# A transformer block on one Trainium2 core: the first residual norm is taken out of the chain to the router

## Chip, cores and metric

One core of one Trainium2 chip runs the whole block as one launch. The metric is device time in microseconds (us), the median of three runs; lower is better. A profile of one execution stands beside the times; all times of instructions below come from it and count from the start of its span.

## The reference, cut to what matters

Sequence 256, width 2048, 32 experts in 4 groups, two experts per token, everything in 32-bit floats.

```python
sh1, sc1, g1, sh2, sc2, g2 = split(silu(c) @ w_ada + b_ada, 6)
u = layer_norm(x) * (1 + sc1) + sh1
mix = token_mixer(u, ...) # attention and gated delta rule, ends in merged @ w_out
x = layer_norm(ALPHA * x + g1 * mix, ln1_g, ln1_b) # the first residual norm
u = layer_norm(x) * (1 + sc2) + sh2 # a second norm, without gain
ffn = hier_moe(u, ...) # router logits u @ [w_group | w_expert], top 2, expert MLPs
x = layer_norm(ALPHA * x + g2 * ffn, ln2_g, ln2_b)
```

So between the projection by `w_out` and the router stand two layer norms, one behind the other, each with a mean and a variance over 2048 columns.

## The kernel before

Tokens lie on the partitions in NT = 2 halves `x[t]` of 128 x 2048. The output projection (`out_todo`) runs over four chunks c of 512 columns; each is 8 half tiles of weights, split into a high and a low part by ScalarE (`wh`) and VectorE (`wl`), and multiplied three times. `evac(c, ps)` takes a finished chunk from PSUM: times the gate row, plus ALPHA times x, statistics by `bn_stats` into `sb`. After chunk 0 it asks for the two rows of the norm, `l1[0]` (gain) and `l1[1]` (bias), each broadcast into a 1 MB buffer; `router_prep` folds the modulation `sc2c` into the router's weights `wr` and `sh2c` into its bias.

After the projection `both` turns the statistics into mean and 1/deviation. Then, for every chunk and half, VectorE normalises x in place (L1059 subtracts the mean and multiplies by the gain, L1060 scales and adds the bias), TensorE transposes the result (L1063), ScalarE copies it out (`uq`) and sums its squares (L1066), and `logits(c)` multiplies it by `wr` (L1053). A copy and a product with `wsel` (L1072, L1075) turn the logits back; small VectorE operations finish the second norm on the logits `L` and choose the experts. ScalarE writes `xh`, the second norm's rows (L1101). For the first pair of experts `slots` makes one-hot columns `G` (L1208), and `gather` multiplies `xh` by them, a quarter (`step(kq)`) of the 16 blocks at a time: two products per block into one PSUM tile, then four modulations into `XT`. Quarter 0 precedes the first `gate_up`; quarters 1 to 3 stand in it ahead of k = 2, 6 and 10 (`GS`).

An expert pair takes 24 weight tiles of 1 MB through the SP queue: 16 for `gate_up`, 8 for `down`. SP issues in order, each load as soon as its buffer is free. There are 17 buffers: 4 (`wp`, L74), 6 (`wm`, L1325) and 7 (`wm1`, L1338). In `wm1` two are first the rows `l1` and five hold the first five gate_up tiles, loaded during the projection (`load_ahead`). Tiles 5 to 8 go to `wp`, 9 to 14 to `wm`, tile 15 and the first six tiles of `down` to `wm1`, and so on round the ring.

The order of instructions on an engine is a planner's: of those ready by its own clock it takes the one that stands first in the program. An instruction that is pinned (`To`, `Vo`, `So`) stays behind the one traced before it on its engine.

Of the kernel before, what the change touches and what calls it, by code (L numbers as in the profile page):

```python
# [37 lines left out]
GS = (2, 6, 10)  # L38
# [25 lines left out]
def tile_block(ctx: ExitStack, tc: tile.TileContext, A: dict, out: bass.AP, dbg=None, upto=99):  # L64
# [855 lines left out]
    rw = rwx.enter_context(tc.tile_pool(name="rw", bufs=1, side=R, reuse_waits="tile"))  # L920
    ahead = []

    def load_ahead():
        n = len(ahead)
        w = wm1.tile([P, 2048], F32, tag="w1", name="w1")
        nc.sync.dma_start(w, A["w_gu"][n])
        ahead.append(w)
# [46 lines left out]
    l1 = []  # L974
# [7 lines left out]
    def router_prep():  # L982
        mod2 = rw.tile([P, KT, 2], F32, name="mod2")
# [5 lines left out]
        V.tensor_tensor(wr, wr, sc2c.unsqueeze(2).to_broadcast([P, KT, 64]), op=MUL)  # L989
        G.memset(wr[:, :, 36:37], 1.0)  # L990
        V.tensor_add(wsel, ident[:, 0:37], ident[:, 64:101])
        rc = rw.tile([36, 2], F32, name="rcol")
        V.tensor_copy(rc, pb[:36, 0:2])
        pb = ps_w.tile([P, 512], F32, tag="ws", name="pbr2")
        for j in range(2):
            T.matmul(pb[:, 64 * j:64 * j + 36], rc[:, j:j + 1].to_broadcast([36, P]), ident[:36, :36],
                     start=True, stop=True)
        V.tensor_tensor(br, pb[:, :36], RI("br"), op=ADD)
        V.tensor_scalar(ncs, pb[:, 64:100], -1.0, None, op0=MUL)

    def g2_rows(cs):
        for c in cs:
            p = ps_w.tile([P, 512], F32, tag="ws", name=f"g2{c}")
            spread(p, mrs[5], 32 * c)
            SC.copy(g2b[:, c * 512:(c + 1) * 512], p)

    def evac(c, ps):
        cs = slice(c * 512, (c + 1) * 512)
        for t in range(NT):
# [15 lines left out]

# [12 lines left out]

    for _ in ada:
        pass  # L1040
    mv, rs = both(sb, "b")
    s2 = mo.tile([P, NT, 4], F32, name="s2")
    nb1 = mo.tile([P, 1], F32, name="nb1")
    V.tensor_reduce(nb1, l1[1], axis=AX.X, op=ADD)
    V.tensor_scalar(nb1, nb1, -1.0 / D, None, op0=MUL)
    pl = ps_w.tile([P, 512], F32, tag="ws", name="pl")
    uqs = []

    def logits(c):
        for k in range(4):  # L1050
            K = 4 * c + k
            j = 64 * (k % 2)
            T.matmul(pl[j:j + 64, :S], wr[:, K, :], uqs[c][:, k, :], start=(K < 2), stop=(K >= KT - 2))  # L1053

    for c in range(4):
        cs = slice(c * 512, (c + 1) * 512)
        uq = rw.tile([P, 4, S], F32, tag="uq", name=f"uq{c}", bufs=2)
        for t in range(NT):
            V.scalar_tensor_tensor(x[t][:, cs], x[t][:, cs], mv[:, t, 0:1], l1[0][:, cs], op0=SUB, op1=MUL)  # L1059
            V.scalar_tensor_tensor(x[t][:, cs], x[t][:, cs], rs[:, t], l1[1][:, cs], op0=MUL, op1=ADD)  # L1060
            p = pg(f"ut{t}{c}")
            for k in range(4):
                T.transpose(p[:, k * P:(k + 1) * P], x[t][:, (4 * c + k) * P:(4 * c + k + 1) * P], ident)  # L1063
            SC.copy(uq[:, :, t * P:(t + 1) * P], p.rearrange("p (k s) -> p k s", k=4))
            scr = rw.tile([P, 512], F32, tag="mt", name=f"sq{c}{t}", bufs=2)
            SC.activation(scr, x[t][:, cs], AF.Square, bias=nb1, accum_out=s2[:, t, c:c + 1])  # L1066
        uqs.append(uq)
        if c:
            logits(c - 1)
    logits(3)  # L1070
    lt = rw.tile([P, S], F32, name="lt")
    SC.copy(lt, pl[:, :S])  # L1072
    pl = ps_w.tile([P, 512], F32, tag="ws", name="plt")
    for t in range(NT):
        T.matmul(pl[:, 64 * t:64 * t + 37], lt[:, t * P:(t + 1) * P], wsel, start=True, stop=True)  # L1075
    for t in range(NT):
        dump(f"x1{t}", x[t])

    mv, dv, sv, rs = [mo.tile([P, NT, 1], F32, name=f"{n}c") for n in ("mv", "dv", "sv", "rs")]
    V.tensor_reduce(sv[:, :, 0], s2, axis=AX.X, op=ADD)  # L1080
    py = pl[:, 0:128].rearrange("p (t c) -> p t c", t=NT)[:, :, 36:37]
    V.tensor_scalar(dv, py, 1.0 / D, nb1, op0=MUL, op1=ADD)
    V.tensor_scalar(mv, py, 1.0 / D, None, op0=MUL)
    V.tensor_tensor(dv, dv, dv, op=MUL)
    V.scalar_tensor_tensor(sv, sv, 1.0 / D, dv, op0=MUL, op1=SUB)
    SC.activation(rs, sv, AF.Sqrt, bias=epsl)
    V.reciprocal(rs, rs)
    for t in range(NT):
        V.scalar_tensor_tensor(L[:, t, :], ncs, mv[:, t, 0:1], pl[:, 64 * t:64 * t + 36], op0=MUL, op1=ADD)
        V.scalar_tensor_tensor(L[:, t, :], L[:, t, :], rs[:, t], br, op0=MUL, op1=ADD)  # L1090
# [9 lines left out]
    for t in range(NT):  # L1100
        SC.activation(xh[t], x[t], AF.Identity, bias=nmr[:, t], scale=rs2[:, t])  # L1101
        g2_rows((2 * t, 2 * t + 1))
# [53 lines left out]
    for t in range(NT):  # L1156
# [4 lines left out]
        V.scalar_tensor_tensor(pos[:, t, :], msk[:, t, :], -4096.0, p[:, :NE], op0=MUL, op1=ADD)  # L1161

# [66 lines left out]
    def gather(pr, Gs):  # L1229
        XT = mo.tile([P, KT, P], F32, tag="XT", name=f"XT{pr}")  # L1230

        def step(kq):
            p = pm(f"xg{pr}_{kq}")
            for k in range(4):
                for t in range(NT):
                    T.matmul(p[:, k * P:(k + 1) * P], xh[t][:, (4 * kq + k) * P:(4 * kq + k + 1) * P],  # L1236
                             Gs[t].bitcast(F32), start=(t == 0), stop=(t == NT - 1))
            for k in range(4):
                K = 4 * kq + k
                if kq % 2:  # L1240
# [359 lines left out]
```

## Time and profile before

| what | us |
|---|---|
| three runs, median (lowest to highest) | 1811.14 (1809.91 to 1812.76) |
| the profiled execution, its own time | 1810.3 |
| its span in the profile | 1808.4 |
| last product of the projection starts | 822.77 |
| first product of the first gate_up starts | 853.05 |

The rows further down come from the page of this execution and from questions to its trace. A row of a timeline has start, length, engine, line, operation, output<-inputs, number of instructions; in brackets the engine's idle time before it and what ended it. PEld is TensorE's weight load; each 32-bit product shows as two records of PE and of PEld.

### The profile page before, as it was taken

The page shows a single profiled execution, that of the slowest core. Times are in us where ns is not written, and L with a number is a line of the kernel's source. Part 1 is how long each engine was busy: PE and PEld are TensorE (multiplying, and loading weights), DVE is VectorE, ACT ScalarE, POOL GpSimd, SP SyncE. Part 2 cuts the span into 40 slices and gives each one's busy share as a digit, 9 for nine tenths or more (in the row PEclk, how much of TensorE's full clock was granted, in tenths as well). Part 3 has the DMA queues.
Part 4 walks back from the last instruction along what each step waited for, and adds up shares of the span by engine and source line. Part 5 has one row for each costly group of instructions (what it writes and reads, how often), then busy time and mean ns, then how long its engine had stood idle before and what let it go on. Part 6 is the DMA issues. An engine that isn't in the chain of part 4 may idle for free. (4 is left out here: it accounts for less than half of the span.)

```text
span 1808.4 us, 27501 instructions
## 1 busy us (share of the span) xinstructions
PE 1726.9 (95%) x11526; PEld 1106.4 (61%) x11526; DVE 895.6 (50%) x1454; ACT 516.9 (29%) x955; POOL 43.4 (2%) x50
## 2 busy tenths in 40 slices
PE   7999998999999999997999999999999999999995
PEld 4779887898999999885434444344434444343331
DVE  3356897798788788666223322233213321233026
ACT  3334798336333544435100110011100110011101
POOL 0000001103000000000000000000000000000000
PEclk8999998999999999999999999999999999999998
DMA  9995565465788688978999999999999999999995
GB/s 397 420 362 209 199 254 192 163 258 205 282 288 319 233 303 317 364 263 323 368 421 420 421 420 420 421 421 420 420 421 420 421 420 421 420 420 421 394 422 223
DMA packets 87287, 628.58 MB, mean 348 GB/s; under 512 B 9828, under 2 KB 9828, under 8 KB 11252
## 3 DMA queue, kind: packets, MB, share of 16 engines
q1 hardware_dynamic: 86832, 626.43, 86.4%
q8 instruction: 92, 1.51, 0.3%
q10 hardware_dynamic: 328, 0.36, 0.1%
q14 instruction: 35, 0.29, 0.0%
HBM read 624.65 MB, written 2.10 MB: 347 GB/s over the span
## 5 line engine op out<-in xcount | busy, mean ns | idle before, releaser
L1257 PE MATMUL pg<-w,XT 128*64 128x512 f32 x1024 | 278.5, 599 | 3.4 <-DMA w<-in_w_gu 2.5
L1257 PE MATMUL pu<-w,XT 128*64 128x512 f32 x1024 | 275.5, 594 | 0.0
L293 PE MATMUL ws<-uh,wh 128*128 128x256 f32 x896 | 259.4, 290 | 2.3 <-ACT wh L288 2.3
L288 ACT CAST wh<-w 128x1024 fp32r<-128x1024 f32 x176 | 184.6, 1050 | 257.3 <-PE ws L294 122.2
L295 PE MATMUL ws<-uh,wl 128*128 128x256 f32 x896 | 254.0, 284 | 4.3 <-DVE wl L289 4.3
L294 PE MATMUL ws<-ul,wh 128*128 128x256 f32 x896 | 253.7, 283 | 0.0
L289 DVE TENSOR_TENSOR wl<-w,wh 128x1024 fp32r<-128x1024 f32 x176 | 218.7, 1243 | 52.4 <-PE mx L294 22.8
L1295 PE MATMUL pd<-w,hT 128*64 128x512 f32 x1016 | 234.1, 599 | 0.8 <-DVE hT L1272 0.8
L1264 DVE TENSOR_TENSOR hs<-hs,pu 128x512 f32<-128x512 f32 x16 | 11.0, 687 | 430.3 <-PE pu L1257 430.3
L293 PEld LDWEIGHTS ws<-uh,wh 128*128 128x128 f32 x896 | 169.3, 189 | 12.4 <-issue 7.8
L295 PEld LDWEIGHTS ws<-uh,wl 128*128 128x128 f32 x896 | 169.1, 189 | 6.6 <-DVE wl L289 5.7
L236 DVE SCALAR_TENSOR_TENSOR acc<-w,csil,acc 128x1024 f32<-128x1024 f32 x128 | 165.3, 1307 | 12.6 <-DMA w<-in_w_ada 12.3
L294 PEld LDWEIGHTS ws<-ul,wh 128*128 128x128 f32 x896 | 169.3, 189 | 1.4 <-issue 1.2
L1257 PEld LDWEIGHTS pu<-w,XT 128*64 128x64 f32 x1024 | 77.8, 137 | 146.6 <-issue 146.6
L1257 PEld LDWEIGHTS pg<-w,XT 128*64 128x64 f32 x1024 | 72.5, 137 | 133.6 <-issue 114.0
L1236 PEld LDWEIGHTS xg<-G,xh 128*128 128x128 f32 x1024 | 120.0, 193 | 41.3 <-issue 25.8
L1295 PEld LDWEIGHTS pd<-w,hT 128*64 128x64 f32 x1016 | 66.4, 136 | 124.1 <-issue 109.2
L1236 PE MATMUL xg<-G,xh 128*128 128x128 f32 x1024 | 131.7, 283 | 6.9 <-DVE x L1312 3.5
L1263 ACT ACTIVATE hs<-pg 128x512 f32<-128x512 f32 x16 | 9.6, 598 | 438.5 <-PE pg L1257 438.5
L410 ACT CAST dh<-pd 128x512 fp32r<-128x512 f32 x64 | 37.6, 587 | 281.3 <-DVE pd L1298 160.8
L1298 DVE SCALAR_TENSOR_TENSOR pd<-pd,wsl,g2b 128x512 f32<-128x512 f32 x64 | 48.5, 758 | 104.0 <-PE pd L1295 104.0
L1312 DVE TENSOR_TENSOR x<-x,cb 128x512 f32<-128x512 f32 x120 | 76.9, 682 | 22.7 <-PE cb L1308 22.7
(391 smaller groups left out, 2363.8 us busy)
## 6 DMA issues: line engine op xcount, KB each, us to landing
w<-in_w_gu SPq DMA_DIRECT2D x256, 1024.0 KB, 19.8
w<-in_w_dn SPq DMA_DIRECT2D x127, 1024.0 KB, 19.8
w<-in_w_ada SPq DMA_DIRECT2D x64, 1024.0 KB, 5.1
w<-in_w_in SPq DMA_DIRECT2D x56, 1024.0 KB, 5.1
wx<-in_w_a SPq DMA_DIRECT2D x18, 1024.0 KB, 11.1
w<-in_w_pab SPq DMA_DIRECT2D x16, 1024.0 KB, 6.0
w<-in_w_out SPq DMA_DIRECT2D x16, 1024.0 KB, 4.9
w<-in_w_a SPq DMA_DIRECT2D x14, 1024.0 KB, 10.7
```

The source lines that it names most:

```text
L236: V.scalar_tensor_tensor(acc[:, hc], w[:, hc], csil[:, k:k + 1], acc[:, hc], op0=MUL, op1=ADD)
L288: SC.copy(h, w)
L289: V.tensor_tensor(lo, w, h.bitcast(F32), op=SUB)
L293: T.matmul(p, a[0], b[0], start=first, stop=False)
L294: T.matmul(p, a[0], b[1], start=False, stop=False)
L295: T.matmul(p, a[1], b[0], start=False, stop=last)
L410: SC.copy(h, src)
L1236: T.matmul(p[:, k * P:(k + 1) * P], xh[t][:, (4 * kq + k) * P:(4 * kq + k + 1) * P], Gs[t].bitcast(F32), start=(t == 0), stop=(t == NT - 1))
L1257: T.matmul(dst[64 * e:64 * e + 64, :], XT[:, k, 64 * e:64 * e + 64], we[:, e * 1024 + hv * 512:e * 1024 + hv * 512 + 512], start=(k == 0), ...
L1295: T.matmul(pd[64 * e:64 * e + 64, :], hT[:, f, 64 * e:64 * e + 64], we[:, (2 * (f % 2) + e) * 512:(2 * (f % 2) + e + 1) * 512], start=(f = ...
L1298: V.scalar_tensor_tensor(pd, pd, ws, g2b[:, cs], op0=MUL, op1=MUL)
L1312: V.tensor_tensor(x[t][:, cs], x[t][:, cs], p, op=ADD)
```

## The change

The first norm is no longer applied before the router. In `evac` every chunk is reduced by the mean of its first chunk, `mu0`, and multiplied by the gain at once; ScalarE sums the squares there. The transposes and logit products are taken from these scaled rows. They are pinned: behind the projection's last product, one chunk and half after the other, each pair of transposes and logits in its turn. The logits are now 39 columns wide with tokens on the partitions: 36 for the router, and three (ones, gain, bias) from which small VectorE operations correct the mean, the deviation and the bias afterwards, with constants `cons` that `router_prep` computes by 16 + 4 more small products, after chunk 0 now. The transposed `lt` and `wsel` go.

`xh` is not written ahead of the first gather. `first_gather` multiplies x by one-hot columns scaled by `ag`, and adds a third product per block: three rows (gain, bias, ones) times `r3`. Behind each quarter VectorE finishes the rows of x with `l1[0]` and `l1[1]` and ScalarE writes `xh` for the other pairs. The quarters stand ahead of k = 1, 3, 5. The five `wm1` buffers for the first gate_up tiles are reserved first, the two for `l1` after them. The rows `g2b` are made ahead of the top-2 choice, not after `xh`.

```diff
-GS = (2, 6, 10)
+GS = (1, 3, 5)
@@
+    early = [wm1.tile([P, 2048], F32, tag="w1", name="w1") for _ in AHEAD]
@@ load_ahead
-        w = wm1.tile([P, 2048], F32, tag="w1", name="w1")
-        nc.sync.dma_start(w, A["w_gu"][n])
+        nc.sync.dma_start(early[n], A["w_gu"][n])
@@ (moved up from evac, c == 0)
+    for q in (0, 4):
+        w = wm1.tile([P, D], F32, tag="w1", name=f"l1{q}")
+        nc.sync.dma_start(w, A["lnr"][q:q + 4, :].rearrange("a b -> (a b)").partition_broadcast(P))
+        l1.append(w)
@@ router_prep
+        for k in range(KT):
+            T.matmul(pb[:39, 0:3], wr[:, k, :39], wr[:, k, 36:39], start=(k == 0), stop=(k == KT - 1))
+        V.tensor_copy(rc[:, 0:3], pb[:39, 0:3])
+        for j in range(4):
+            T.matmul(pb[:, 64 * j:64 * j + 39], rc[:, j:j + 1].to_broadcast([39, P]), ident[:39, :39],
+                     start=True, stop=True)
@@ new
+    def turn_part(c, t):
+        uqs[c, t] = rw.tile([P, 4, P], F32, tag="uq", name=f"uq{c}{t}", bufs=4)
+        p = ps_w.tile([P, 512], F32, tag="ws", name=f"ut{t}{c}")
+        for k in range(4):
+            To.transpose(p[:, k * P:(k + 1) * P], x[t][:, (4 * c + k) * P:(4 * c + k + 1) * P], ident)
+        SC.copy(uqs[c, t], p.rearrange("p (k s) -> p k s", k=4))
+
+    def logits(c, t):
+        for k in range(4):
+            K = 4 * c + k
+            To.matmul(pt[t], uqs[c, t][:, k, :], wr[:, K, :39], start=(K == 0), stop=(K == KT - 1))
@@ evac
+            if c == 0:
+                V.bn_aggr(mu0[:, t, :], sb[:, t, 0:1])
+            V.scalar_tensor_tensor(x[t][:, cs], x[t][:, cs], mu0[:, t, 0:1], l1[0][:, cs], op0=SUB, op1=MUL)
+            SC.activation(mt, x[t][:, cs], AF.Square, accum_out=s2[:, t, c:c + 1])
@@ after the projection
+    for i, u in enumerate(units_):
+        turn_part(*u)
+        if i == 4:
+            mv, rs = both(sb, "b")
+        if i:
+            logits(*units_[i - 1])
+    logits(*units_[-1])
     for _ in ada:
         pass
+    g2_rows(range(4))
@@ 15 small VectorE operations, then
+    SC.activation(rs2, sv, AF.Sqrt, bias=epsl)
+    stt(lambda t: L[:, t, :], lambda t: cons[:, 0, :36], nm, lambda t: pa[:, t, :36])
+    V.reciprocal(rs2, rs2)
+    stt(lambda t: L[:, t, :], lambda t: L[:, t, :], rs2, lambda t: br)
@@
-    for t in range(NT):
-        SC.activation(xh[t], x[t], AF.Identity, bias=nmr[:, t], scale=rs2[:, t])
-        g2_rows((2 * t, 2 * t + 1))
+    G.memset(xh[1][:3], 1.0)
+    nc.scalar.dma_start(xh[1][:2], A["lnr"][0:8].rearrange("(q c) b -> q (c b)", q=2))
@@ new, for pair 0
+    def first_gather(Gs):
+        for t in range(NT):
+            V.tensor_scalar(Gp[:, t], Gs[t].bitcast(F32), ag[:, t], None, op0=MUL)
+        for t in range(NT):
+            To.matmul(p[:3, :P], vk[:, t], Gs[t].bitcast(F32), start=(t == 0), stop=(t == NT - 1))
+        SC.copy(r3, p[:3, :P])
+        def products(p, kq, k):
+            for t in range(NT):
+                To.matmul(p, x[t][:, K], Gp[:, t], start=(t == 0), stop=False)
+            To.matmul(p, xh[1][:3, K], r3, start=False, stop=True)
+        def step(kq):
+            ...
+            for t in range(NT):
+                V.scalar_tensor_tensor(x[t][:, cs], l1[0][:, cs], nd[:, t], x[t][:, cs], op0=MUL, op1=ADD)
+                V.scalar_tensor_tensor(x[t][:, cs], x[t][:, cs], rsb[:, t], l1[1][:, cs], op0=MUL, op1=ADD)
+                SC.activation(xh[t][:, cs], x[t][:, cs], AF.Identity, bias=nmr[:, t], scale=rs2[:, t])
@@ gate_up
-                    T.matmul(dst[64 * e:64 * e + 64, :], XT[:, k, 64 * e:64 * e + 64],
+                    (To if step is not None and k < 8 else T).matmul(dst[64 * e:64 * e + 64, :], XT[:, k, 64 * e:64 * e + 64],
```

## Rows read from the trace of the kernel before

**Rows 1.** The page, the span in 40 equal slices: busy share of the DMA engines in tenths, and what they moved.

```profile
DMA  9995565465788688978999999999999999999995
GB/s 397 420 362 209 199 254 192 163 258 205 282 288 319 233 303 317 364 263 323 368 421 420 421 420 420 421 421 420 420 421 420 421 420 421 420 420 421 394 422 223
```

**Rows 2.** Stretches of 5 us: from:to, length, then busy time (and instructions) of PE, PEld, DVE, ACT, POOL, the granted clock of TensorE as a share of 2.4 GHz, the DMA engines' busy share, GB/s.

```profile
845.00:850.00 5.00, 2.60 (x19) 2.23 (x18) 2.66 (x22) 4.98 (x4) 0.00 (x0) 0.98 0.47 193
850.00:855.00 5.00, 4.50 (x22) 3.05 (x23) 1.55 (x10) 2.50 (x8) 0.00 (x0) 0.68 0.01 2
855.00:860.00 5.00, 5.00 (x30) 2.28 (x28) 1.37 (x4) 0.00 (x0) 0.00 (x0) 1.00 0.74 270
...
895.00:900.00 5.00, 5.00 (x41) 4.21 (x42) 2.79 (x9) 1.51 (x4) 0.00 (x0) 1.00 0.50 210
900.00:905.00 5.00, 5.00 (x26) 1.72 (x24) 2.35 (x7) 0.59 (x1) 0.00 (x0) 1.00 0.58 226
...
1780.00:1785.00 5.00, 4.85 (x22) 1.73 (x20) 3.83 (x6) 0.45 (x2) 0.00 (x0) 1.00 0.44 179
```

**Rows 3.** Timeline of the SP queue, the issues of weight loads around the first pair of experts, asked in short stretches: start, us spent issuing, line, load.

```profile
835.94 0.33 SPq L1338 DMA_DIRECT2D w<-in_w_gu  x1
837.26 0.33 SPq L1338 DMA_DIRECT2D w<-in_w_dn  x1
855.11 0.33 SPq L1338 DMA_DIRECT2D w<-in_w_dn  x1
856.82 0.33 SPq L1338 DMA_DIRECT2D w<-in_w_dn  x1
...
865.15 0.33 SPq L74 DMA_DIRECT2D w<-in_w_dn  x1
869.00 0.33 SPq L74 DMA_DIRECT2D w<-in_w_dn  x1
...
886.58 0.33 SPq L1338 DMA_DIRECT2D w<-in_w_gu  x1
900.73 0.33 SPq L1338 DMA_DIRECT2D w<-in_w_gu  x1
```

**Rows 4.** Timeline of all engines between the projection's end and the first gate_up, in order of time.

```profile
823.09 1.06 PE L241 MATMUL ada<-acc,cst 128*32 128x512 f32 x8
...
829.20 2.74 DVE L1060 SCALAR_TENSOR_TENSOR x<-x,rsb,l 128x512 f32<-128x512 f32 x4
...
830.00 3.29 PE L1063 MATMUL ut<-cst,x 128*128 128x128 f32 x16 [5.85 <-DVE x L1060]
...
837.15 0.86 PEld L1063 LDWEIGHTS ut<-cst,x 128*128 128x128 f32 x8 [0.38 <-issue]
...
840.15 0.37 ACT L1072 COPY lt<-pl 128x256 f32<-128x256 f32 x1 [0.52 <-PE pl L1053]
...
841.25 0.22 DVE L1082 TENSOR_SCALAR dvc<-plt,nb 128x2 f32<-128x2 f32 x1 [1.43 <-PE plt L1075]
...
841.74 0.16 DVE L1085 SCALAR_TENSOR_TENSOR svc<-svc,dvc 128x2 f32<-128x2 f32 x1
...
842.46 0.42 DVE L1090 SCALAR_TENSOR_TENSOR L<-L,rsc,br 128x36 f32<-128x36 f32 x2
...
848.24 4.31 PE L1236 MATMUL xg<-G,xh 128*128 128x128 f32 x22 [0.57 <-DVE G L1208]
...
848.82 3.44 PEld L1236 LDWEIGHTS xg<-G,xh 128*128 128x128 f32 x20 [0.31 <-ACT xh L1101]
...
852.54 1.51 ACT L1244 ACTIVATE XT<-xg,sh2c,sc2c 128x128 f32<-128x128 f32 x4
...
853.05 1.15 PE L1257 MATMUL pg<-w,XT 128*64 128x512 f32 x4 [0.50 <-ACT XT L1244]
...
858.13 1.37 DVE L1241 TENSOR_SCALAR XT<-xg,sc2c,sh2c 128x128 f32<-128x128 f32 x4 [5.23 <-PE xg L1236]
```

**Rows 5.** Timeline of TensorE inside and just behind the first gate_up: a gather quarter, and products of 32 columns with 128 x 128 weights.

```profile
865.04 2.05 PE L1236 MATMUL xg<-G,xh 128*128 128x128 f32 x16
867.02 1.08 PE L1257 MATMUL pg<-w,XT 128*64 128x512 f32 x4
...
886.47 0.63 PE L1195 MATMUL cnt<-msk,cst 128*128 128x32 f32 x4
886.94 0.41 PE L1219 MATMUL gt<-cst,G 128*128 128x128 f32 x2
```

**Rows 6.** Timeline of TensorE where chunk 0 of the projection has ended and VectorE is at `evac`.

```profile
756.42 0.61 PE L293 MATMUL mx<-wh,mh 128*128 128x512 f32 x2
756.87 1.02 PE L168 MATMUL g<-mr,cst 128*128 128x512 f32 x2
757.82 1.28 PE L988 MATMUL pbr<-mod,rin 128*36 128x2 f32 x32
759.03 0.50 PE L294 MATMUL mx<-wl,mh 128*128 128x512 f32 x1
```

**Rows 7.** Timeline of VectorE at the same place: the weight splits that follow `evac`.

```profile
757.03 2.35 DVE L289 TENSOR_TENSOR wl<-w,wh 128x1024 fp32r<-128x1024 f32 x2
```

**Rows 8.** The page's list of the costliest groups, the casts of the weight splits: busy time, mean ns of one, then ScalarE's idle time just before them and what ended most of it.

```profile
L288 ACT CAST wh<-w 128x1024 fp32r<-128x1024 f32 x176 | 184.6, 1050 | 257.3 <-PE ws L294 122.2
```

**Rows 9.** The page's list of DMA issues: KB each, median us from issue to landing.

```profile
out<-x SPq DMA_DIRECT2D x2, 256.0 KB, 2.5
```

More of the change, by code (lines that the diff above doesn't have):

```diff
@@ L924, in load_ahead @@
         n = len(ahead)
-        w = wm1.tile([P, 2048], F32, tag="w1", name="w1")
-        nc.sync.dma_start(w, A["w_gu"][n])
-        ahead.append(w)
+        nc.sync.dma_start(early[n], A["w_gu"][n])
+        ahead.append(early[n])
     def out_todo():
@@ L960, in tile_block @@
     sb = mo.tile([P, NT, 4, 6], F32, name="sb")
+    s2 = mo.tile([P, NT, 4], F32, name="s2")
+    mu0 = mo.tile([P, NT, 2], F32, name="mu0")
+    nb1 = mo.tile([P, 1], F32, name="nb1")
     g2b = mo.tile([P, D], F32, name="g2b")
@@ L988, in router_prep @@
             T.matmul(pb[:36, 0:2], wr[:, k, :36], mod2[:, k, :], start=(k == 0), stop=(k == KT - 1))
-        V.tensor_tensor(wr, wr, sc2c.unsqueeze(2).to_broadcast([P, KT, 64]), op=MUL)
+        rc = rw.tile([39, 4], F32, name="rcol")
+        G.memset(rc, 0.0)
+        V.tensor_copy(rc[:36, 3:4], pb[:36, 0:1])
+        V.tensor_tensor(wr[:, :, :36], wr[:, :, :36], sc2c.unsqueeze(2).to_broadcast([P, KT, 36]), op=MUL)
         G.memset(wr[:, :, 36:37], 1.0)
-        V.tensor_add(wsel, ident[:, 0:37], ident[:, 64:101])
@@ L1024, in evac @@
             router_prep()
+        if c == 2:
+            SC.activation(epst, epsl, AF.Sqrt)
+    epst = mo.tile([P, 1], F32, name="epst")
     g1_row(0)
@@ L1037, in both @@
         return mv, rs
+    pt = [pg(f"pl{t}")[:, :39] for t in range(NT)]
+    units_ = [(c, t) for c in range(4) for t in range(NT)]
+    for i, u in enumerate(units_):
[5 more added lines that the diff above has]
+    logits(*units_[-1])
     for _ in ada:
         pass
[L1041 to L1057, printed above, removed]
-        for t in range(NT):
[L1059 to L1073, printed above, removed]
-    for t in range(NT):
[L1075 to L1090, printed above, removed]
@@ new lines, in stt @@
+    def stt(dst, a, sc, b):
+        for t in range(NT):
+            V.scalar_tensor_tensor(dst(t), a(t), sc[:, t], b(t), op0=MUL, op1=ADD)
+    one = lambda a: (lambda t: a[:, t])
+    col = lambda j: (lambda t: pt[t][:, j:j + 1])
+    pcol = lambda j: (lambda t: pa[:, t, j:j + 1])
+    stt(one(q2), col(37), nd, one(sv))
+    stt(one(pa), lambda t: cons[:, 1], nd, lambda t: pt[t])
+    stt(one(pa), one(pa), rs, lambda t: cons[:, 2])
+    stt(one(q2), one(q2), rs, col(38))
+    V.tensor_scalar(nm, pa[:, :, 36:37], -1.0 / D, None, op0=MUL)
@@ L1248, in gate_up, with spread_out @@
+    def spread_out(XT, p, kq):
+        for k in range(4):
+            K = 4 * kq + k
+            if kq % 2:
+                V.tensor_scalar(XT[:, K, :], p[:, k * P:(k + 1) * P], sc2c[:, K:K + 1], sh2c[:, K:K + 1],
+                                op0=MUL, op1=ADD)
+            else:
+                SC.activation(XT[:, K, :], p[:, k * P:(k + 1) * P], AF.Identity, bias=sh2c[:, K:K + 1],
+                              scale=sc2c[:, K:K + 1])
     def gate_up(pr, XT, load, step=None):
@@ L1440, in tile_block @@
             Gs = slots(pr, pair(pr)[0])
-            XT, step = gather(pr, Gs)
+            XT, step = first_gather(Gs)
             step(0)
```

67 lines of the change are left out of this document (40 added, 27 removed).

## Prediction

> **What bounds the kernel now.** I read the DMA lines of the page first, then the stretches of 5 us, then the SP queue, and only then the engines. From slice 21 on the DMA engines are at 9 tenths or more and move 420 to 421 GB/s in almost every slice [rows 1]: the experts' part is paced by weight loads, 1 MB tiles at 1.0486 MB / 420 GB/s = 2.5 us each. Nothing that TensorE wins there counts in itself; what counts is time in which the DMA engines have nothing to move. After the projection there are two such holes [rows 2]. The first: share 0.47, 0.01, 0.74 in three stretches, so dry from about 847.4 to 856.3. The second: 0.50 and 0.58, so from about 897.5 to 902.1. Then they run to about 1782.2 (share 0.44), and 26 us of last products and last norm follow.
>
> Why dry? SP stands at a load whose buffer is still in use. The two `l1` buffers come free when the norm has been applied, and SP fills them at 835.94 and 837.26; the next buffer is that of gate_up tile 0, free at 855.11 [rows 3]. This ends the first hole (855.11 plus about 1.2 us until bytes move, by the share 0.74). The second ends at 900.73, when `down` has used its first tile and the load of tile 9 of the next pair (call it N9) may go. After N9 nothing is dry any more. So **the end is set by the time at which N9 starts to move: 902.0 now**. It can't start before its buffer is free, and not before the loads queued ahead of it have gone.
>
> **The change, part by part.** Call the start of the first gate_up product g; now 853.05 [rows 4]. First the shift of g.
>
> A. Projection. TensorE paces it. `router_prep` adds 16 products of 39 weight columns; the like of them took 759.03 - 757.82 = 1.2 us [rows 6]. Four instead of two turning products add 4 records at (886.94 - 886.47) / 4 = 0.118 [rows 5], 0.5 us. In `evac` VectorE has per chunk two more passes at 2.74 / 4 = 0.69 [rows 4], 1.4 us, and in chunk 0 two small aggregations. Just there the next weight split waits behind `evac`: at 757.03 to 758.2 [rows 7], while TensorE fills its wait with a gate row and `pbr`, from 756.87 to 759.03 [rows 6]. 1.7 us more minus 0.8 us of cover is a stall of 0.9 us. Chunks 1 and 2 have no such fill; each costs from nothing (the split is put ahead) to the 1.4 us. Bounds: 0.8 us (products fill the stalls) and 4.0; I take 2.5. ScalarE's squares, two more passes a chunk, I cost at nothing: it stands idle 257.3 / 176 = 1.5 us ahead of each cast [rows 8]; if that cover went, the casts `wh` would be late next.
>
> B. Transposes and logits. Before, TensorE waits 5.85 us for the normalised rows [rows 4] and the last logits leave PSUM at 840.15. After, it can start at 823.09 and is the pace itself: eight units, each 8 transpose records (0.86 us with their tail, I take 0.9) [rows 4] and 8 logit records at 0.118 = 0.94 [rows 5]. 8 x 1.84 = 14.7, plus 0.3 of drain: 838.1. B = -2.0. Bounds: -3 (1.7 us per unit) and +0.3 (2.1 per unit, with the 8 `ada` records, 0.45 us, put between).
> These rows have 32 moving columns and 128 weight columns, like the new logits' 39 and 128, so the price is taken over as it is. [...]
>
> C. Last logits to experts. Before, 840.15 to 841.25 for the copy and the `wsel` product, 0.65 us of statistics to the end of L1085, then 0.98 for square root, reciprocal and L [rows 4]. After, no copy, but 15 small operations at about 0.11 (between L1082 and L1085 four start in 0.49 us): 0.15 + 1.65 + 0.98 = 2.8 against 2.73. C = 0, from -0.3 to +0.4.
>
> D. New small work on VectorE around the choice (three scalars, two scaled copies of G): at 0.11 to 0.25 each, +0.4 to +0.8; I take +0.6.
>
> E. First gather. Before, 22 records from 848.24, loads at 3.44 / 20 = 0.172; XT starts at 852.54 [rows 4]. After, no wait for `xh`, but 4 + 24 records ahead of XT. At 0.172 (granted clock 0.68 in 850 to 855, so partly at the lower of its two levels, 1.2 GHz, after idling [rows 2]) that is 4.8 us, at 0.124 (865.04 to 867.02 for 16 [rows 5]) 3.5. Taken 4.2: 852.4 plus drain. E = 0, from -0.7 to +0.8. The copy of r3 hides behind the first block's two products. The two rows loaded into `xh` need a memset and a load, at least the 2.5 us of [rows 9]; they are hidden behind the choice, 842.9 to 848.2, unless that load queues.
>
> g moves by 2.5 - 2.0 + 0 + 0.6 + 0 = **+1.1 us, to 854.2**, bounds 850.3 to 859. The 5.85 us wait that goes is spent again: on pinned transposes that no longer overlap anything, and on more products.
>
> F. Inside the first gate_up. Tile 0 is released at g + 2.06; a further tile costs 1.71, with a quarter ahead of it 3.85 [rows 3]. A quarter now has 24 records: 8 x 0.124 more, 4.84. Quarters ahead of k = 1, 3, 5 release tiles 1 to 6 at g + 6.9, 8.6, 13.5, 15.2, 20.0, 21.7. The third products have three rows, but 128 weight columns and 128 moving ones, so I count them in full. [...] If they were free, the three quarters would be 3 us shorter.
>
> G. The buffers. This is the dear part. `l1` is now needed until quarter 3 has been finished. SP no longer gets two early buffers, so after ten loads the DMA engines are dry some 5 us earlier, near 842.4 and until g + 3.3. Then in ring order: tile 15 (moves at g + 3.3), down tiles d0 (8.1), d1 (10.6), d2 (14.7), d3 (17.2 to 19.7). d4 goes into `l1[0]`. Quarter 3's products end at g + 15.2 + 3.0 = 18.1; its XT is on VectorE, 1.37 [rows 4], then four passes of 0.69: `l1[0]` is read last at g + 21.6, `l1[1]` at g + 22.3. So d4 moves at g + 22.9; from there 13 tiles back to back (d4 to d7, N0 to N8) take 32.5, and **N9 moves at g + 55.4**. Its buffer is free at 900.73 - 853.05 = 47.7, plus 3.0 for longer quarters, plus 0.7 for the six records of quarter 1 that no longer run ahead: g + 51.4, with 1.2 g + 52.6. It is no longer the buffer but the queue that sets N9.
>
> Sum: 854.2 + 55.4 = 909.6 against 902.0, **+7.6 us**. The profiled execution took 1810.3, the median is 0.8 above it: 1811.1 + 7.6, less 0.7 because chunks 1 and 2 of A stand at their dear end, is 1818.
>
> **Rivals.** *Slower, but only by g and F.* If SP takes loads for freed `wp` buffers ahead of d4, or `l1` is freed sooner, N9 goes at g + 52.6: 906.8, +4.8 us, 1816. For it: the planner may reorder SP; against: no load of [rows 3] overtook another. *Same.* The chain does shrink: A at 0.8, B at -3, E at -0.7 give g = 850.3 and +3.7 with G, +0.9 without, 1812 to 1815. It would need every term at its end, or a smaller stall and one of G's waits gone. [...] *Slower by far.* The 8 `ada` records, unpinned and later in the program, fall behind the pinned logits, so five `wm` loads wait until 838 and the two small rows for `xh` queue behind them until about 852, 3 us late: 1821.
>
> **Chances.** A change of under 0.2% (3.6 us) can't be told from none here. The forecast with G 0.45, its dear version 0.12, the rival by g and F 0.20, same 0.16, faster 0.07. Parts of the first three fall under 3.6 us or out of it: slower 0.74, same 0.18, faster 0.08. Range 1812 to 1823: from g's lower end without G's wait to g's upper bound with it (859 - 854.2 = 4.8 above 1818).
>
> **What would show it.** In the changed trace: the projection's end near 825.6; transposes and logits without gaps, some 14.7 us; first gate_up near 854; SP issuing one load at g + 2 and then standing before `l1` until about g + 21.7; the DMA share near 0 from before 845 to about 857, and again low near g + 20 to 23; no hole left near 900. I am wrong if g comes before 850, or if SP has loads to issue between 843 and g.

## The result, and the profile after

The changed kernel takes 1829.58 us (median of 4 runs, 1828.90 to 1833.77) against 1810.53 beside it: ratio 1.0112, 95% interval 1.0097 to 1.0127. It is 19 us slower; forecast were 7.6, with a range that ended at 1823. The profiled execution took 1829.99 us, its span is 1828.2.

First the stretches of the changed kernel as in [rows 2].

```profile
850.00:855.00 5.00, 1.41 (x7) 1.30 (x8) 3.89 (x35) 1.49 (x2) 0.19 (x2) 0.82 0.92 383
855.00:860.00 5.00, 5.00 (x18) 3.50 (x18) 1.76 (x11) 0.61 (x3) 0.00 (x0) 0.50 0.02 8
860.00:865.00 5.00, 4.45 (x16) 2.87 (x17) 2.68 (x4) 1.53 (x5) 0.00 (x0) 0.50 0.00 0
865.00:870.00 5.00, 5.00 (x24) 2.51 (x20) 0.06 (x1) 1.38 (x2) 0.00 (x0) 0.81 0.34 87
870.00:875.00 5.00, 5.00 (x25) 2.17 (x24) 4.01 (x8) 0.81 (x1) 0.00 (x0) 1.00 0.39 143
...
885.00:890.00 5.00, 5.00 (x27) 2.66 (x28) 3.40 (x8) 0.71 (x1) 0.00 (x0) 1.00 0.64 247
...
900.00:905.00 5.00, 5.00 (x26) 1.71 (x24) 0.00 (x0) 0.00 (x0) 0.00 (x0) 1.00 1.01 423
...
915.00:920.00 5.00, 5.00 (x40) 4.02 (x41) 2.78 (x10) 1.50 (x4) 0.00 (x0) 1.00 1.01 415
920.00:925.00 5.00, 5.00 (x26) 1.58 (x22) 2.02 (x5) 0.59 (x1) 0.00 (x0) 1.00 1.01 421
```

The eighth figure (granted clock, as a share of full speed) and the two behind it (DMA share, GB/s) tell it. The clock has two levels in the traces of before and after, 1.00 and 0.50; a figure between them is a stretch with both. From 855 to 865 TensorE is busy in nearly all of the time, at 0.50 of its clock, the lower level, and nothing is loaded. The DMA engines are dry for more than 10 us, then starved, with one break, until 890; before, the hole was 9 us long and had ended at 856. The second hole of before, near 900, is gone, as forecast. The dry time has moved to the front.

The SP queue, asked in short stretches as in [rows 3]:

```profile
832.23 0.33 SPq L1386 DMA_DIRECT2D w<-in_w_gu  x1
840.46 1.98 SPq L1386 DMA_DIRECT2D w<-in_w_gu  x4
867.38 0.33 SPq L1399 DMA_DIRECT2D w<-in_w_gu  x1
873.46 2.04 SPq L1399 DMA_DIRECT2D w<-in_w_dn  x2
881.26 2.04 SPq L1399 DMA_DIRECT2D w<-in_w_dn  x2
889.07 0.33 SPq L74 DMA_DIRECT2D w<-in_w_dn  x1
889.94 1.12 SPq L1399 DMA_DIRECT2D w<-in_w_dn  x2
...
906.24 0.33 SPq L1399 DMA_DIRECT2D w<-in_w_gu  x1
920.38 0.33 SPq L1399 DMA_DIRECT2D w<-in_w_gu  x1
```

The last line is N9, at 920.38 instead of 900.73. Tile 0 comes free at 867.38, and a tile with a quarter ahead of it takes 6.08 us (867.38 to 873.46), where before it took 3.85 [rows 3] and 4.84 was forecast. The first two lines are `wm` loads: one that goes at once, and four of the five behind it, which wait 7.8 us for the late `ada` products.

When N9 has landed is asked of its load alone, first before (issued at 900.73), then after (920.38):

```profile
DMA to landing us min/median/max: 4.8/4.8/4.8
DMA to landing us min/median/max: 7.0/7.0/7.0
```

Before, the queue was empty and N9 landed at 905.5. After, N8, the load of 906.24, lands 18.7 us behind its issue, at 924.9; N9 lands at 927.4, 2.5 us behind it, and the DMA share is 1.01 in both stretches around (915 to 925). So N9's own buffer was free while loads ahead of it were still moving.

TensorE between the projection and the first gate_up, as in [rows 4]:

```profile
831.80 0.39 PE L295 MATMUL mx<-wh,ml 128*128 128x512 f32 x1
832.03 1.04 PE L150 MATMUL ut<-cst,x 128*128 128x128 f32 x8
...
853.02 0.91 PE L1179 MATMUL rk<-msk,cst 128*128 128x32 f32 x4 [4.67 <-DVE msk L1159]
...
854.93 1.01 PE L150 MATMUL rk<-G,vk 128*3 128x128 f32 x4 [0.58 <-DVE G L1235]
855.87 1.22 PE L150 MATMUL xg<-Gp,x 128*128 128x128 f32 x4
857.02 0.79 PE L150 MATMUL xg<-r,xh 3*128 3x128 f32 x2
...
863.98 1.98 PE L150 MATMUL pg<-w,XT 128*64 128x512 f32 x4 [0.55 <-ACT XT L1306]
```

The 5.85 us wait is gone, the transposes start at once. But g is 863.98, and the first gather (854.93 to g) takes 9.05 us instead of 4.81.

The following table takes the profiled executions of all kernels apart, by the trace, in us. "Start" is the first product of the projection; up to there TensorE's instructions are the same, and it still lies anywhere from 728.8 to 735.2. So what a change does is best read from there on. The stages: the projection (first to last product), then to the end of the last logits, then to the first product that takes G, then to g, then to the span's end.

| kernel | start | projection | logits | choice | first gather | g to end | start to end | median |
|---|---|---|---|---|---|---|---|---|
| before | 730.61 | 92.2 | 17.3 | 8.1 | 4.8 | 955.3 | 1077.8 | 1810.5 |
| after | 733.25 | 98.55 | 13.9 | 9.2 | 9.05 | 964.2 | 1094.9 | 1829.6 |
| a_fill | 729.54 | 98.5 | 13.9 | 8.8 | 8.5 | 964.5 | 1094.2 | 1824.9 |
| a_cons | 732.68 | 93.2 | 16.2 | 8.25 | 9.06 | 964.8 | 1091.4 | 1826.3 |
| a_free | 734.18 | 98.6 | 13.9 | 9.4 | 9.06 | 969.7 | 1100.6 | 1831.8 |
| a_no3 | 729.54 | 98.5 | 13.9 | 9.4 | 5.2 | 957.7 | 1084.6 | 1816.5 |
| a_no3_free | 732.03 | 98.5 | 13.9 | 9.4 | 5.3 | 956.6 | 1083.7 | 1814.4 |
| a_k128 | 729.63 | 97.0 | 13.9 | 9.4 | 6.15 | 960.8 | 1087.2 | 1818.6 |
| a_fill_k128 | 735.22 | 96.9 | 13.9 | 8.8 | 4.0 | 959.7 | 1083.3 | 1819.6 |
| a_all | 728.81 | 93.1 | 22.9 | 9.6 | 4.05 | 958.8 | 1088.5 | 1821.1 |
| b_gs | 729.37 | 92.2 | 18.3 | 8.1 | 4.8 | 954.8 | 1078.1 | 1810.3 |
| b_hold | 731.31 | 92.2 | 18.1 | 15.2 | 4.2 | 954.9 | 1084.5 | 1816.7 |
| b_late | 733.86 | 92.2 | 17.3 | 8.1 | 3.0 | 955.2 | 1075.9 | 1810.5 |
| b_fill_late | 732.04 | 92.2 | 18.0 | 8.1 | 4.0 | 955.8 | 1078.1 | 1810.3 |

After against before: +6.4 - 3.45 + 1.1 + 4.2 + 8.9 = +17.2 (rounded), and 2.6 more from the start.

### The profile page after: what moved, and what is told of

Read it like the earlier page. It is cut to its first block, busy times and chain, and to the rows that moved or that the text cites. A ratio compares the mean times of both kernels' runs of the same rounds, so it can differ in the third digit from the quotient of the medians.

```text
span 1828.2 us, 27736 instructions
## 1 busy us (share of the span) xinstructions
PE 1747.7 (96%) x11626; PEld 1124.0 (61%) x11626; DVE 902.4 (49%) x1481; ACT 517.7 (28%) x962; POOL 47.1 (3%) x55
## 5 line engine op out<-in xcount | busy, mean ns | idle before, releaser
L1318 PE MATMUL pg<-w,XT 128*64 128x512 f32 x992 | 269.5, 598 | 4.9 <-DMA w<-in_w_gu 4.5
L1318 PE MATMUL pu<-w,XT 128*64 128x512 f32 x992 | 266.4, 592 | 0.0
L1263 PEld LDWEIGHTS xg<-G,xh 128*128 128x128 f32 x960 | 111.4, 191 | 37.8 <-issue 22.7
L1263 PE MATMUL xg<-G,xh 128*128 128x128 f32 x960 | 122.0, 281 | 6.1 <-DVE x L1373 3.5
```

The lines of the kernel that those rows point to most:

```text
L1318: (To if step is not None and k < 8 else T).matmul(dst[64 * e:64 * e + 64, :], XT[:, k, 64 * e:64 * e + 64], we[:, e * 1024 + hv * 512:e * ...
```

## Experiments

**The third products: a_no3 and a_k128.** a_no3 leaves them out:

```
-                To.matmul(p, x[t][:, K], Gp[:, t], start=(t == 0), stop=False)
-            To.matmul(p, xh[1][:3, K], r3, start=False, stop=True)
+                To.matmul(p, x[t][:, K], Gp[:, t], start=(t == 0), stop=(t == NT - 1))
```

> The changed kernel without the third product per block in the first gather (left out: the rows gain, bias and ones times r3). Theory (a third product costs what the trace after shows, 0.42 us at full and 0.72 us at half clock): first gather 2.9 us shorter, each of three quarters 1.7 us, together 8 us less, about 1821.6. Rival (it costs as predicted, 8 records of 0.124 a quarter): 1.4 + 3 x 1.0 = 4.4 us less, about 1825.

1816.47 us (1816.02 to 1817.30), ratio 1.0028 (1.0012 to 1.0044): 13.1 us come back, more than either expected; the profiles show 10.3 of them from the start on. a_k128 keeps them and gives them 128 rows, 125 of them zeros in `r3`: the same sum.

```
-    G.memset(xh[1][:3], 1.0)
+    G.memset(xh[1], 1.0)
...
+        G.memset(r3, 0.0)
+        SC.copy(r3[:3], p[:3, :P])
...
-            To.matmul(p, xh[1][:3, K], r3, start=False, stop=True)
+            To.matmul(p, xh[1][:, K], r3, start=False, stop=True)
```

> The changed kernel with the third product of the first gather over all 128 rows: xh's other rows are set to one, r3's other rows to zero, so the sum is the same. Theory (products that fill three rows of the array pass for no activity and let the clock fall, and switching between three rows and 128 costs extra): the first gather falls from 8.1 to 3.5 to 5 us, the first tile by 1.2, each of the three quarters by about 1.1: 7 to 8 us less, about 1822. Rival (a product costs by its weight columns, and the clock is low only because TensorE idled before): nothing changes, 1829.6.

1818.56 us (1815.75 to 1822.17), ratio 1.0049 (1.0025 to 1.0072): 11.0 us come back with not one instruction less on TensorE. Not all of them are the rows: from the start on the profile is 7.8 us shorter, 2.9 in the first gather, 3.4 behind g and 1.6 in the projection, which this edit doesn't touch (the clock was low there for half as long, see a_cons); the start lay 3.6 us earlier. A gather quarter within gate_up, first in the changed kernel, then in a_k128, both at full clock:

```profile
868.32 0.71 PE L150 MATMUL xg<-Gp,x 128*128 128x128 f32 x4
868.96 0.48 PE L150 MATMUL xg<-r,xh 3*128 3x128 f32 x2
869.37 0.71 PE L150 MATMUL xg<-Gp,x 128*128 128x128 f32 x4
```

```profile
858.67 0.61 PE L150 MATMUL xg<-Gp,x 128*128 128x128 f32 x4
859.12 0.39 PE L150 MATMUL xg<-r,xh 128*128 128x128 f32 x2
859.35 0.61 PE L150 MATMUL xg<-Gp,x 128*128 128x128 f32 x4
```

Read the starts. With three rows the third product holds TensorE for 869.37 - 868.96 = 0.41 us and the pair beside it for 0.64; with 128 rows 0.23 and 0.45. Record by record, the extra tenths lie next to the change between row counts. With 128 rows throughout (a_k128), every record starts 0.11 us behind the one before. In the changed kernel so do the middle ones of the four full records; the last full one ahead of the third product takes 0.205 from start to start, the third product's two 0.214 and 0.200, the first full one behind it 0.213. Products of 39 rows and 128 weight columns, eight records in a row, start 0.11 to 0.13 apart, and only the last, ahead of 128 rows, takes 0.21 (a_cons, 833.05 to 834.06). So in these traces the records next to a change of row count pay, and in the rows of a_k128 above none does; what more than two three-row records in a row cost was not run.

A tile with a quarter ahead takes 4.75 us then (858.01 to 862.76 on the SP queue), near the forecast's 4.84.

**The clock: a_fill and a_fill_k128.** Five products into an unused PSUM tile, pinned ahead of L, keep TensorE busy while VectorE chooses:

```
+    pf = pg("fill")
+    for j in range(5):
+        To.matmul(pf, ident, l1[0][:, :512], start=True, stop=True)
     dump("L", L.rearrange("p t c -> p (t c)"))
```

> The changed kernel with five idle products (512 columns each, 0.85 us) on TensorE behind the g2 rows, into a PSUM tile that nobody reads, to bridge its idle time while the experts are chosen. Theory (clock): the first gather and the first gate_up tile ran at 1.2 GHz because TensorE had idled 848.4 to 853.0; bridged, 28 records take about 0.176 us instead of 0.30 (saves 3.5 us) and the first tile 2.1 instead of 3.3 us (1.2 us): about 4.8 us less, 1825. Rival (the third products wait for r3 and are slow in themselves): the first gather stays near 8.5 us and the time at 1829.6.

1824.92 us (1822.86 to 1830.66), ratio 1.0086 (1.0061 to 1.0111). The 4.7 us look like a hit, but the profile doesn't show them: from its start on a_fill takes 1094.2 against 1094.9, and the first gather is hardly shorter. The clock was up when the gather began and then fell:

```profile
850.00:852.00 2.00, 1.42 (x10) 0.87 (x9) 1.17 (x7) 0.36 (x2) 0.00 (x0) 1.00 0.38 152
852.00:854.00 2.00, 1.68 (x6) 1.43 (x6) 1.20 (x8) 0.25 (x1) 0.00 (x0) 0.50 0.04 8
854.00:856.00 2.00, 2.00 (x8) 1.43 (x6) 0.00 (x0) 0.00 (x0) 0.00 (x0) 0.50 0.00 0
```

a_fill_k128 has the same filler and 128 rows.

> The changed kernel with five idle products of 512 columns ahead of L and with third products over all 128 rows. Theory (clock and short products are two separate losses of the first gather): the first gather falls from 5.2 us (a_k128) to the 3.5 us of a_all, and the rank product to first gather by 0.9 us (a_fill): 1818.6 - 2.6 = 1816.0 us. Rival (a_fill's gain was mostly the place of its profile in the scatter): 1818.5 us.

Here the clock stays up through the gather, which takes 4.0 us (3.5 from the first product with `x`):

```profile
855.00:857.00 2.00, 2.00 (x18) 1.75 (x17) 1.23 (x9) 0.36 (x2) 0.00 (x0) 1.00 0.06 20
857.00:859.00 2.00, 1.45 (x15) 1.26 (x15) 1.52 (x5) 0.86 (x3) 0.00 (x0) 1.00 0.00 0
```

So both together kept the upper level (1.00 from 849 to 861), and with three rows the filler alone did not (0.50 from 852 to 862). What the chip counts as activity, as the theory of a_k128 has it, no run shows; the runs show the level beside the row count. The kernels without the filler say the same. With no third products or with 128 rows the low stretch around the gather lasted 6.8 us and ended ahead of g (a_no3, a_k128). With three rows it lasted 13.7 us (after, a_cons) or 27.3 (a_free), past g each time, as it did in a_fill (10.2 us). (In a_fill TensorE also waited 0.33 us for the two rows of `xh` early in the gather.) In time the gain isn't there: 1819.56 us (1814.08 to 1820.94), ratio 1.0045 (1.0030 to 1.0059), no less than a_k128, though its profile is 3.8 us shorter from its start on. The start of this profile lies 5.6 us later than in a_k128's, and runs of one kernel scatter by 7. Whether the filler pays in time isn't decided.

**The constant products: a_cons and a_all.** The 16 products that the change added to `router_prep`, and its four turning ones, go out of the projection, to behind the fourth unit of transposes:

```
-            router_prep()
+            rcs.append(router_prep())
...
+        if i == 3:
+            router_consts(rcs[0])
```

> The changed kernel with the 16 + 4 new constant products of router_prep taken out of the projection and pinned among the first transposes behind it. Theory (small products and the stall around them drop TensorE's clock inside the projection, 763 to 771): the stretch from the gate row of chunk 1 to the last product falls from 76.4 us to 70 to 72, 2.6 us come back behind it, net 3 to 4 us less, about 1826. Rival (the two longer passes of evac on VectorE stall the projection): the stretch stays above 75 us and the time rises by 2 us to about 1831.5.

1826.28 us (1822.93 to 1836.48), ratio 1.0101 (1.0064 to 1.0139). The projection takes 93.16, 5.4 less, and the logits 2.3 more. The passes and squares of `evac` cost no more than about 1.5: 93.16 - 92.16 = 1.0, and 0.5 for the two turning products of before that left with the others. What made up the 5.4 is seen in the changed kernel, at the place of [rows 6]:

```profile
760.45 0.61 PE L293 MATMUL mx<-wh,mh 128*128 128x512 f32 x2
762.32 1.33 PE L1008 MATMUL pbr<-rin 128*39 128x3 f32 x32 [1.26 <-ACT mt L1049]
763.58 0.51 PE L294 MATMUL mx<-wl,mh 128*128 128x512 f32 x1
764.02 1.53 PE L1012 MATMUL pbr<-cst,rcol 39*128 39x39 f32 x8
765.48 0.79 PE L295 MATMUL mx<-wh,ml 128*128 128x512 f32 x1
766.07 0.63 PE L294 MATMUL mx<-wl,mh 128*128 128x512 f32 x1
766.50 0.63 PE L295 MATMUL mx<-wh,ml 128*128 128x512 f32 x1
...
771.48 0.40 PE L295 MATMUL mx<-wh,ml 128*128 128x512 f32 x1
```

```profile
766.00:768.00 2.00, 2.00 (x6) 1.54 (x5) 0.13 (x1) 0.00 (x0) 0.00 (x0) 0.50 0.67 279
```

The 32 records take 1.26 us. The eight turning ones take 1.46, but 1.01 where the clock stays up (a_cons, 833.05 to 834.06 below): it fell among them. Then TensorE, full of wide products, runs at the lower level: a record each 0.43 us (766.07 to 766.50) instead of 0.227. From 765.48 to 771.48 there are 14 records; at 0.227 they take 3.2 of these 6.0 us, so 2.8 are the clock's, and with the 0.45 of the turning ones 3.3. 1.26 + 1.01 + 3.3 = 5.6, close to a_cons. Two other runs agree: in a_k128 and a_fill_k128 the low stretch lasted 3.4 us instead of 6.8, and their projection is 1.6 us shorter. The clock fell at this place in all seven kernels that have these products there (projection 96.9 to 98.6 us), and in none of the seven others (92.2 to 93.2). The last wait of TensorE ahead of the fall is the 1.26 us in the first rows; a_cons has one of 0.68 us there and stays at 1.00. In a_cons' own profile the moved products, too, left the clock at 1.00. a_all (filler, moved products and 128 rows) shows that this is no rule:

> The changed kernel with three repairs at once: idle products while the experts are chosen, the constant products out of the projection, third products over 128 rows. If the causes are separate, 3 us (constants) and 5 us (idle products) and some 6 us of the third products add up: about 1815 to 1816. If they are the same loss counted twice, 1821 or more. By either it stays slower than the kernel before.

1821.07 us (1819.13 to 1824.92), ratio 1.0074 (1.0052 to 1.0095): 2.5 us above a_k128 alone, with overlapping intervals. The gather takes 4.05 us, as at the upper level in a_fill_k128 (4.0), but behind the same products in the same place the clock now falls among the logits (0.50 from 831 to 848), though TensorE had been busy without a break since 822. TensorE in a_cons, then in a_all:

```profile
833.05 1.08 PE L150 MATMUL pbr<-cst,rcol 39*128 39x39 f32 x8
834.06 1.08 PE L150 MATMUL pl<-rin,uq 128*128 128x39 f32 x8
834.98 0.63 PE L150 MATMUL ut<-cst,x 128*128 128x128 f32 x4
```

```profile
829.13 1.08 PE L150 MATMUL pbr<-cst,rcol 39*128 39x39 f32 x8
830.14 1.44 PE L150 MATMUL pl<-rin,uq 128*128 128x39 f32 x8
831.37 1.09 PE L150 MATMUL ut<-cst,x 128*128 128x128 f32 x4
```

The logits take 22.9 us in a_all and 16.2 in a_cons.

**Holding `l1`: a_free, a_no3_free, b_gs, b_hold.** a_free drops the two passes that read `l1` in each quarter, so SP may refill it early (the kernel leaves the rows for the later pairs unfinished).

```
-                V.scalar_tensor_tensor(x[t][:, cs], l1[0][:, cs], nd[:, t], x[t][:, cs], op0=MUL, op1=ADD)
-                V.scalar_tensor_tensor(x[t][:, cs], x[t][:, cs], rsb[:, t], l1[1][:, cs], op0=MUL, op1=ADD)
```

> The changed kernel without the two VectorE passes per quarter that finish x with l1[0] and l1[1] (left out, so later pairs see unfinished rows): l1 is free before the first gather, as in the kernel before. By step G of the prediction N9 would no longer wait for the queue behind d4: about 6 us less, 1823.5. Rival, from the changed kernel's trace: N9's own buffer comes free only 1 us before its turn in the queue, so at most 1.2 us less, 1828.4 to 1829.6.

1831.84 us (1829.31 to 1836.55), ratio 1.0114 (1.0097 to 1.0131): no gain. But this run doesn't price the hold. In its profile, the slowest of its four runs, the clock stayed at the lower level until 881, 14 us longer than in the changed kernel:

```profile
875.00:880.00 5.00, 5.00 (x15) 1.96 (x16) 1.37 (x4) 0.81 (x1) 0.00 (x0) 0.50 0.00 0
```

So N9's own buffer came free 62.4 us behind g (issue at 927.46) instead of 56.4, the DMA engines ran dry ahead of it (share 0.36 from 925 to 930), and what the early `l1` might have gained can't be read. a_no3_free does the same to a_no3, where TensorE is faster.

> The changed kernel without its third products (as in a_no3) and also without the two passes per quarter that read l1, so that later pairs work on unfinished rows and l1 comes free ahead of the first gate_up. In a_no3 the end lies 957.7 us behind the first gate_up product (1814.2 - 856.49), in b_gs, where l1 is free early, 954.8 (1807.5 - 852.74); N9's own buffer is only 0.8 us of these 2.9 (issue at g + 49.8 against g + 49.0). Theory (step G: where TensorE is at full clock the queue behind l1 sets N9, and that is the other 2.1 us): 1816.5 - 2.1 = 1814.4 us, and the DMA share shows a hole near 900 again. Rival (holding l1 costs nothing, as a_free says): 1816.5 us.

1814.43 us (1811.33 to 1817.93), ratio 1.0020 (1.0009 to 1.0031), against 1816.47 for a_no3. The hole before N9 is back. Stretches of a_no3, then of a_no3_free:

```profile
905.00:910.00 5.00, 5.00 (x26) 1.61 (x24) 2.80 (x9) 0.59 (x1) 0.00 (x0) 1.00 1.01 416
```

```profile
905.00:910.00 5.00, 5.00 (x35) 2.98 (x35) 2.41 (x9) 1.38 (x4) 0.00 (x0) 1.00 0.16 33
```

So in a_no3 the queue behind `l1` did set N9: it lands 56.9 us behind g there, 7.1 behind its issue, and in a_no3_free 54.6 behind g, 4.8 behind its issue. The price is 1.1 us by "g to end", 2.0 by the medians and 1.4 by the ratios; the intervals overlap, so the traces show the wait and the times don't settle its size. The try from the other side failed. b_gs puts the quarters of the kernel before ahead of tiles 1, 3, 5:

```
-GS = (2, 6, 10)
+GS = (1, 3, 5)
```

> The kernel before with GS = (1, 3, 5) alone. Every theory: the quarters' products only change place, N9's buffer is free at the same time, so 1811 as before, within 1 us. It is the base for the run that holds l1.

1810.28 us (1808.00 to 1812.49), ratio 1.0004 (0.9994 to 1.0014): no difference. b_hold adds to this the early reservation of the five tiles, as in the change, and four idle passes per quarter that read `l1` (shown alone):

```
+            if pr == 0:
+                cs = slice(512 * kq, 512 * kq + 512)
+                for t in range(NT):
+                    V.scalar_tensor_tensor(hx, l1[0][:, cs], nmr[:, t], x[t][:, cs], op0=MUL, op1=ADD)
+                    V.scalar_tensor_tensor(hx, hx, rs2[:, t], l1[1][:, cs], op0=MUL, op1=ADD)
```

> The kernel before with the l1 buffers alone treated as in the change: the five early tiles reserved first, quarters ahead of k = 1, 3, 5, and four VectorE passes per quarter that read l1[0] and l1[1] and write a scratch tile. Step G of the prediction, in this kernel's own times: d4 moves near g + 20.5, N9 near g + 53 instead of g + 49: 3 to 4 us slower than the same kernel without the hold. Rival: SP always finds another free buffer, at most 1 us.

1816.65 us (1813.16 to 1822.54), ratio 1.0038 (1.0022 to 1.0053), 6.4 more than b_gs, but not for the hold. The planner put the passes, which wait for nothing, among the small steps of the choice; VectorE:

```profile
844.47 0.74 DVE L1250 SCALAR_TENSOR_TENSOR hx<-l,nmr,x 128x512 f32<-128x512 f32 x1
845.13 0.35 DVE L1130 SCALAR_TENSOR_TENSOR og<-L,mg,cst 128x4 f32<-128x4 f32 x2
...
845.47 0.74 DVE L1251 SCALAR_TENSOR_TENSOR hx<-hx,rsc,l 128x512 f32<-128x512 f32 x1
```

Thirteen of the sixteen passes start inside the choice, which takes 15.2 us instead of 8.1; the last starts at 859.11 and ends a microsecond ahead of g, and "g to end" is unchanged. So the run says what such work inside the choice costs, and nothing of an `l1` that is held past g.

**Can the kernel before gain from this?** There, too, the first gather runs at the lower level in part [rows 2], and the cast of `combp` waits 1.54 us on ScalarE just ahead of XT. b_late moves the routing weights behind the first XT; b_fill_late also adds two idle products behind the last `g2` row.

```
+            weights()
             hs = gate_up(pr, XT, lambda k: gu_load(pr, k), step)
-            weights()
...
-        SC.activation(eg, eg, AF.Exp)
+        So.activation(eg, eg, AF.Exp)
```

(the last line in both; the filler as in a_fill, with two products that read `mrs[5]`)

> The kernel before with the routing weights computed behind the first gate_up's products in the program and their exponential pinned behind the first XT, so that ScalarE's cast of combp, which waited 1.54 us at 852.39 for comb, no longer stands ahead of the first XT at 852.54. Theory: the first gate_up starts 0.5 to 1.0 us earlier and the end follows: 1809.3 us. Rival (XT waits for the gather's products anyway): 1810.1 us.

> b_late and two idle products of 512 columns behind the last g2 row, where TensorE idles from 845.1 to 846.8 and the granted clock then falls to 0.50 in 850 to 853. Theory (the first gather runs at the upper level, 3.5 us instead of 4.3, and the clock costs about another 0.5 us in the rank products): 1810.1 - 2.0 = 1808.1 us. Rival (TensorE's clock there is set by later idling, from 847.4 on, which the two products don't touch): as b_late, 1809.3 us or more.

1810.54 us (1807.57 to 1812.43, ratio 1.0002, 0.9993 to 1.0010) and 1810.28 (1806.48 to 1812.83, ratio 0.9995, 0.9985 to 1.0004): no difference. In b_late's profile the gather did fall to 3.0 us at the upper level (1.00 from 846 to 856), and 1.9 us were gained from the start on, yet 12 runs don't bear it out. In b_fill_late's profile the gain went into a wait for the normalised rows, the very thing that the change removes:

```profile
851.89 2.50 PE L1239 MATMUL xg<-G,xh 128*128 128x128 f32 x20 [1.06 <-ACT xh L1101]
```

No version here beats the kernel before.

## Why the prediction was right in sign and too small

**The bound** was read rightly: TensorE's gain in the logits bought nothing, and the end follows N9. N9 is issued 19.65 us later in the trace, the span is 19.8 longer. The landing is the sharper sign. In six of the seven profiles in which N9 waits its turn behind N8 the end lies 900.8 us behind N9's landing (902.3 in a_k128); where N9's own buffer is the last thing waited for, before among them, it lies 901.1 to 902.8 behind. So N9 lands 21.9 us later after the change, and 2.0 of these don't reach the end.

**B** was right in kind: -3.5 instead of -2.0, a little past its bound of -3, with the transposes starting at 832.03 behind the last product at 831.80. No row gives the 1.7 us per unit of that bound; in the changed kernel a unit with nothing between its products took 1.28 (834.89 to 836.17). **C and D** together +1.1 for +0.6.

**A failed in size:** +6.4 for 2.5, bounds 0.8 to 4.0. The products were sized about rightly: 1.26 us for "the like of them took 759.03 - 757.82 = 1.2 us", and 1.01 / 8 = 0.126 at full clock for the turning ones at 0.118. What the sum lacks is the clock. It takes every product at the upper level, and the lower one cost 3.3 us, among and behind these products. `evac`, on which I spent most of A, is 1 to 1.5; in the changed kernel TensorE waits in the projection once, 1.26 us just ahead of the constant products. With this wait, and less the 0.5 that two turning products took before, that is 6.3 of the 6.4.

**E failed:** the first gather went from 4.81 to 9.05, forecast no change, with +0.8 as the bound. Two things, both shown: the three-row products cost 0.41 and slow their neighbours, 0.4 us a block at full clock (a_k128 has neither), and they run wholly at the lower level (a_fill_k128 doesn't). I had taken a price between the two levels because the gather of before had seen both; behind 4.67 us of idling it started at the lower one, and with three rows it left it only at 866.9, behind g (863.98). No trace shows a clock in GHz: for the 1.2 GHz of E and of the expectation of a_fill the measured figure is the share of 0.50, and what [rows 2] gives is a share of full speed.

**F failed by the same sentence:** "The third products have three rows, but 128 weight columns and 128 moving ones, so I count them in full." They cost more than in full. A weight load alone did cost the same with few rows: a record of it took 0.18 us with 3 rows and 0.19 with 128 (after, 867 to 871). The whole product did not: 0.41 us with 3 rows against 0.23 with 128 (a_k128) at the same columns, where row counts change from product to product.

**G was right in its reason and, at full rows, in its offset.** Forecast was N9's own buffer at g + 51.4 and the queue as the later bound, by 2.8 us. The buffer came at g + 56.4: 51.4, plus three quartered tiles at 6.08 - 4.84 = 1.24, plus 1.34 for the first tile (867.38 - 863.98 = 3.40 instead of 2.06), whose products run at the lower level, is 56.5. The load into `l1[0]` was issued at 889.94, g + 26.0, so it could move near g + 27.2 instead of 22.9; one of the tiles behind it had overtaken it (L74 at 889.07). The queue was the later bound, as forecast: N9 landed 7.0 us behind its issue, where it took 4.8 in before with nothing ahead of it, so by 2.2 us. In a_no3, too, it is by 2.3 (7.1 against 4.8), of which 1.1 show in "g to end" once `l1` is free (a_no3_free). For the changed kernel itself no run shows what an early `l1` would give back, since a_free's clock went another way.

So the sum holds for another kernel than the one that was run: a_k128, whose third products do cost "in full", has 1818.56 us against a forecast of 1818, though terms cancel in it (A +4.8, B -3.5, first gather +1.3). That it meets the forecast is in part luck. Of the other 11 us (11.4 between the two profiles) the traces put 6.3 on the three rows, in the first gather and behind g; 1.6 are the clock in the projection and 3.6 the start. The rival "slower by far" named a different mechanism; its held `wm` loads are there (7.8 us ahead of 840.46), and with them the DMA engines stayed busy until 855, where the forecast had them dry from 842.4. SP then stood before tile 0's buffer until 867.38, so in this trace N9 doesn't seem to follow from the hold; no experiment priced it. Wrong in the chances: they add up to 1 over outcomes of which none lies above 1823, and left nothing for TensorE's price for a shape the trace of before didn't have, nor for a clock that stays low.

## What to carry to other kernels

A product over a few rows wasn't cheap here, small as its sum is: between products over all rows the one with 3 rows took 0.41 us and the same sum padded with zeros to 128 rows 0.23. So pad it if the tile allows it and measure, or price it by a row of the same shape in the same company, and if the trace has none, keep the range open upward. A sum over TensorE's products also needs a term for the clock: here small products (after, from 764.5) and 4.67 us of idling (after, from 853.2) were each followed by time at 0.50, 6.8 and 13.7 us. The 5.85 us wait is gone here and the kernel is 19 us slower, because the last load that has to wait is issued 19.65 us later: follow the chain to that load before pricing anything else. Whether it waited for its buffer or for its turn was told by its time from issue to landing, 4.8 us in before and 7.0 in after. When medians of a few runs and one profile disagree by some us, compare the profiles from the first instruction that differs; where the runs scatter as much, leave the size open.

## What the runs showed of the hardware

- A product with 3 rows (fp32, 128 weight columns, 128 moving ones) between products with 128 rows took 0.41 us where the one with 128 rows took 0.23, and the pair of full products next to it 0.64 instead of 0.45. The extra lay in the records next to a change of the row count (0.20 to 0.21 us from start to start instead of 0.11); among eight 39-row records in a row (0.11 to 0.13, a_cons) there was none until the last (0.21).
- The granted clock stayed at 0.50 while TensorE was busy or nearly so: with three-row products in the stream (a_fill, 852 to 862; a_free, 854 to 881; with 128 rows in the same places it stayed at 1.00 in a_fill_k128) and behind small products of 39 rows or columns (after, 766 to 770: 0.427 us instead of 0.227 for wide products; a_all, 831 to 848).
- The same small products in the same place left the clock at 1.00 in one kernel's profile (a_cons) and not in another's (a_all). What decides between them stays open.
- A 1 MB load that found the queue empty landed 4.7 to 5.1 us behind its issue (N9 in before, a_free, a_no3_free and the four b_ kernels); one that waited its turn landed about 2.5 us behind the load ahead of it (after, 924.9 and 927.4).
